# A gMLP/Hyena encoder block on one core: skip taps in fp32r, adaLN work of the filter stage on GpSimd and ScalarE, low halves on VectorE, and two output groups evicted tile by tile

## The chip, the cores and the metric

The kernel runs on 1 core of one Trainium2 chip. The metric is device time in microseconds (us) of one execution. Engine names are those of the profile: PE is TensorE's matmul (PEld its weight load), DVE is VectorE, ACT is ScalarE, POOL is GpSimd, SP is SyncE, which only issues DMAs here. A few DMAs are issued from ACT's queue.

## The reference

One layer on x of 512 x 2048, float32:

```
mod = SiLU(c) @ W_ada + b_ada -> sh1, sc1, g1, sh2, sc2, g2      (adaLN)
h   = x * (1 + sc1) + sh1
z   = h @ W_in + b_in      -> gMLP u, v | Hyena v, x1, x2 | gates a, b
A   = gMLP spatial gating of (u, v);  B = Hyena: y = x2 * (h2 * (x1 * (h1 * v)))
mix = (sigmoid(g_a) * (A @ W_a) + sigmoid(g_b) * (B @ W_b)) @ W_o + b_o
x   = LN(alpha * x + g1 * mix)
x   = LN(alpha * x + g2 * MLP_relu2(x * (1 + sc2) + sh2))
```

The Hyena's long filters h1, h2 (two directions each) come from a small network: two layers with Sin on 33 features, a third layer w3, a decay window. They are applied as convolutions by Fourier transforms; each filter has a `skip` term that is added to its first tap.

## The kernel before, in words

**Precision by pairs.** A large product is made of three fp32r matmuls: every operand is split into a high part (rounded to fp32r by a copy on ACT) and a low part (the difference, a subtraction on DVE): hi x hi, hi x lo, lo x hi. `split` (L74) does both halves. Weights come in blocks of 128x1024 (`wraw`), go through a ring of three buffers, and are split by `Weights.cast` (L164, ACT) and `Weights.finish` (L169, DVE). A dense group is eight blocks of 24 matmuls; before each block it takes a split pair of the ring, after each block it runs the functions listed for that block in `stages`.

**The order of work** is written out by hand: every engine runs its instructions in the order of the program, and waits where an operand is missing. An instruction that waits holds up all that is queued behind it on its engine.

**The opening (0 to about 190 us)** holds three threads, interwoven.

1. *adaLN vectors.* `Modulation` streams W_ada in 192 raw blocks of 128x1024. `step` (L289) is one DVE instruction per block: multiply by SiLU(c) (`cond`) and sum into `dots`. Four blocks give the shift and scale of one 128-row slice of the input; `load` asks for a further block with each step. The first 64 blocks are needed in the opening.
2. *The input.* After every fourth step `first_input` (L471) adds up `mod` (two tiny sums, L295 and L296, on POOL), makes the high part and the full value of h for this slice on ACT (L476, L477), and the low part on POOL (L478). Sixteen slices make h.
3. *The filters.* After the two Sin layers (`Sine`, `ready`) a loop of eight parts runs `taps(n+1)` (12 fp32r matmuls, L435, and in every second part one fp32 matmul with one row, `first_tap` x `skip`, L437), `transform(n)` (six fp32 matmul products, L338), two adaLN steps, `windowed(n+1)` (four DVE products that read PSUM, L445), the splitting of the next w3 half (`parts`), and the transform's `sums` (six DVE operations). `busy` puts dummy transposes on PE: 10, then 14 and 14 in the opening.

Then the first two dense groups of W_in (Hyena's v) run interleaved in 16 rounds: adaLN steps (44 in 13 rounds), `weights.finish` for the block of the next round, 24 matmuls, `weights.cast`.

**The output projection (from 1128 us).** Groups 0 and 1 of w_o (512 columns each) run on all four tiles of 128 tokens, groups 2 and 3 first on the two early tiles, then on the two late ones. `token_dense` returns four (or two) PSUM banks of eight; `gated_1` (L957) evicts each tile with three DVE operations (L960 times the gate row, L961 into the residual, L962 statistics) after the group's last matmul.

Of the kernel before, what the change touches and what calls it, by code (L numbers as in the profile page):

```python
# [18 lines left out]
P = 128  # L19
# [21 lines left out]
def block_kernel(ctx: ExitStack, tc: tile.TileContext, t):  # L41
# [25 lines left out]
    def f32(ap):  # L67
        return ap.bitcast(F32)
# [184 lines left out]
    nc.gpsimd.memset(sign[HID:], -1.0)  # L253
    first_tap = const.tile([1, P], F32, name="first_tap")
    nc.gpsimd.memset(first_tap, 0.0)
    nc.gpsimd.memset(first_tap[:, 0:1], 1.0)
    ident = const.tile([P, P], F32, name="ident")
# [12 lines left out]
    class Modulation:  # L270
        def __init__(self, order, room=lambda: 0):

            self.order, self.raw, self.room = [(m, kc, h) for m, kc in order for h in range(2)], [], room

        def load(self):
            early = sum(r[0] for r in self.raw)
            more = early < min(self.room(), 8)
            if self.order and (more or len(self.raw) - early < 3):
                m, kc, h = self.order.pop(0)
                if more:  # L280
                    raw = actp.tile([P, 1024], F32, name="araw", tag="act")
                else:
                    raw = wts.tile([P, 1024], F32, name="araw", tag="araw")
                load(raw, t["ada"][m, kc, h])
                self.raw.append((more, raw, m, kc, h))

        def step(self):
# [3 lines left out]
            if len(self.raw) < 11:  # L291
                self.load()

    def mod_sum(m, kc, eng=nc.vector):
# [91 lines left out]
    class Filters:  # L386
# [6 lines left out]
        def middle(self):  # L393
            x = self.one.reduce()
            nc.scalar.activation(x, x, AF.Sin)
            self.two = Sine(hw2, x, 1, P)

        def ready(self):

            x = self.two.reduce()  # L400
            nc.scalar.activation(x, x, AF.Sin)
            even, odd = slot_pair("a2e"), slot_pair("a2o")
            split(x, *even)
            for a, b in zip(even, odd):
                nc.scalar.activation(b, f32(a), AF.Identity, scale=sign)
            self.a2 = [[a.rearrange("h (p k) -> h k p", k=4) for a in pair] for pair in (even, odd)]

        def fetch(self, n):

            o, hf, cs = PARTS[n]  # L410
            if cs == 0:
                w = load(slot("w3"), t["w3"][o, hf].rearrange("d h c -> (d h) c"))
                skip = load(slot("skip")[:1], t["skip"][o, hf:hf + 1])
                self.raw.append((w, skip))
            if n in (0, 2):
# [3 lines left out]
        def parts(self, n):  # L419
            if PARTS[n][2] == 0:  # L420
                w, skip = self.raw.pop(0)
                both = slot_pair("w3")
                split(w, *both)
                self.w.append((*both, skip))

        def taps(self, n):

            cs = PARTS[n][2]
            wh, wl, skip = self.w[0] if cs == 0 else self.w.pop(0)
            ah, al = self.a2[cs]  # L430
            for cl in range(4):
# [4 lines left out]
                if extra:  # L436
                    nc.tensor.matmul(ps, first_tap, skip, start=False, stop=True)  # L437
                self.ps.append(ps)
# [31 lines left out]

    def first_input(kc, xt):  # L471

        mod_sum(slice(0, 2), kc, nc.gpsimd)
        hi, lo = act_pair(kc)
        sc, sh = mod[:, 1, kc:kc + 1], mod[:, 0, kc:kc + 1]
        nc.scalar.activation(hi, xt, AF.Identity, bias=sh, scale=sc)  # L476
        nc.scalar.activation(xt, xt, AF.Identity, bias=sh, scale=sc)  # L477
        nc.gpsimd.tensor_tensor(lo, xt, f32(hi), op=OP.subtract)  # L478
        h1.append((hi, lo))
# [22 lines left out]
    flt = Filters()  # L502
    flt.fetch(0)
    silu = [slot("silu") for _ in range(4)]
    quarters = [cond[:, 512 * h:512 * (h + 1)] for h in range(4)]
# [14 lines left out]

    def ada_steps(n):

        for _ in range(n):
            ada.step()
            done.append(None)
            if len(done) % 4 == 0:
                first_input(len(h1), xt[len(h1)])
                x_load()

    x_load()  # L530
# [4 lines left out]
    busy(14)  # L535
    ada_steps(2)
    flt.parts(0)
    flt.ready()
    busy(14)
    x_load()  # L540
    for _ in range(5):
        ada.load()
    flt.taps(0)
    ada_steps(2)
    flt.windowed(0)
    weights.later, weights.queue = [], nc.scalar
    for n in range(8):
        if n < 6 and n % 2 == 0:
            flt.fetch(n + 2)
        if n < 7:  # L550
            flt.taps(n + 1)
        sums = flt.transform(n)
        ada_steps(2)
        if n < 7:
            flt.windowed(n + 1)
        flt.store()
        if n < 6:
# [471 lines left out]
    def norm_stages(tiles, first):  # L1029

        out = {first: [lambda: mom[tiles].append(moments(st1, tiles)), do(normal_1, mom[tiles], tiles, 0)]}
        for k in range(1, 4):
# [3 lines left out]
    residual_load(0)  # L1036
    gated_1(token_dense(w_o, 0, 8, mp, stages={1: [gate_rows], 3: [gate_loads], 4: [do(residual_load, 1)],
                                               5: [do(residual, 0)]}), 0)
    gated_1(token_dense(w_o, 1, 8, mp, stages={0: [do(residual, 1), do(residual_load, 2)], 3: [do(residual, 2)],
                                               4: [do(residual_load, 3)], 6: [do(residual, 3)]}), 1)  # L1040
    for tiles in (early, late):
        for c in (2, 3):
# [5 lines left out]
            elif tiles is late:  # L1048
                stages = {1 + n: [do(second_input, early, 2 * n, held)] for n in range(7)}
            gated_1(token_dense(w_o, c, 8, mp, tiles, stages), c, tiles)  # L1050

# [187 lines left out]
```

## Time and profile before

| | |
|---|---|
| median of 3 runs | 2732.48 us (2732.22 to 2733.73) |
| profiled execution: time, span | 2733.2 us, 2731.4 us |
| mean granted TensorE clock | 0.996 |
| PE busy | 2688.6 us (98%) |
| DVE busy | 1539.5 us (56%) |
| ACT busy | 777.8 us (28%) |
| POOL busy | 118.8 us (4%) |
| DMA | 400.49 MB, mean 147 GB/s |

A line of the profile names the start, the length, the engine, the line of the kernel (L435), the operation, and what is written from what, with shapes. A bracket at the end gives the idle time of the engine before it and what ended it. Busy times of PE include time in which a matmul waits in its pipeline, so PE's start times, one after another, tell more than its share. The chain of waits follows the work that ended last back to the start.

### The profile page before, as it was taken

The numbers are of one execution on the slowest core, as the hardware profiler recorded it, in microseconds if no ns is written. First come the engines' busy times: TensorE is split into PE (matmuls) and PEld (weight loads), VectorE is DVE, ScalarE is ACT, GpSimd is POOL, SyncE is SP. The second block draws the span as 40 slices with busy tenths as digits, with TensorE's granted clock in tenths as the row PEclk, the third lists the DMA queues.
The fourth block names the chain that finished last, engine by engine and source line by source line (L and its number), as shares of the span: only waits on it lengthen the run. The fifth ranks groups of instructions, "written<-read, shape, count | busy, mean of one in ns | idle before, by whom it ended". The sixth has DMA issues, their size and how long they took to land.

```text
span 2731.4 us, 30019 instructions
## 1 busy us (share of the span) xinstructions
PE 2688.6 (98%) x12019; PEld 2210.1 (81%) x12019; DVE 1539.5 (56%) x2052; ACT 777.8 (28%) x949; POOL 118.8 (4%) x102
## 2 busy tenths in 40 slices
PE   8999999999999999999999999999999999999996
PEld 5678778888888888878988888888888888888885
DVE  8987989544575566456774343443433434334348
ACT  2343332222232222324621222312223222131232
POOL 0330000000000000140010000000000000000001
PEclk9999999999999999999999999999999999999998
DMA  9762333555665567445543222322223222223342
GB/s 346 300 242 84 118 113 135 196 190 196 200 209 186 198 220 258 156 152 177 183 134 100 94 100 93 101 93 100 94 99 97 96 100 93 101 92 101 95 140 82
DMA packets 120189, 400.49 MB, mean 147 GB/s; under 512 B 14187, under 2 KB 14283, under 8 KB 119920
## 3 DMA queue, kind: packets, MB, share of 16 engines
q1 hardware_dynamic: 116656, 387.26, 41.9%
q10 hardware_dynamic: 3392, 11.31, 1.1%
q8 instruction: 94, 1.54, 0.2%
q14 instruction: 47, 0.39, 0.0%
HBM read 388.01 MB, written 10.50 MB: 146 GB/s over the span
## 4 chain that ended last, share of the span: by engine, by line
PE 91%; DVE 5%; DMA 3%; issue 1%; ACT 1%; SPq 0%; DVEq 0%; ACTq 0%
PE d L207 57%; PE t L952 29%; DMA araw<-in_ada 2%; PE flt L435 1%; PE f_o L338 1%; DVE wlo L169 1%; DMA spec<-spec 1%; PE inv L703 1%; PE inv L690 1%; DMA wraw<-in_w_m 0%; PE f L342 0%; DVE araw L289 0%; DVE r L1104 0%; DVE r L968 0%; PE tr L609 0%
## 5 line engine op out<-in xcount | busy, mean ns | idle before, releaser
L207 PE MATMUL d<-act,whi 128*128 128x512 f32 (+1 forms) x4224 | 1273.1, 384 | 0.0
L169 DVE TENSOR_TENSOR wlo<-wraw,whi 128x1024 fp32r<-128x1024 f32 x480 | 589.0, 1229 | 993.2 <-ACT whi L164 989.9
L164 ACT CAST whi<-wraw 128x1024 fp32r<-128x1024 f32 x480 | 504.9, 1053 | 1488.2 <-PE d L207 873.2
L207 PEld LDWEIGHTS d<-act,whi 128*128 128x128 f32 x4224 | 783.1, 188 | 155.6 <-issue 2.4
L207 PE MATMUL d<-act,wlo 128*128 128x512 f32 (+1 forms) x2112 | 810.2, 384 | 10.2 <-DVE wlo L169 10.2
L207 PEld LDWEIGHTS d<-act,wlo 128*128 128x128 f32 x2112 | 396.7, 188 | 93.3 <-DVE wlo L169 15.9
L952 PE MATMUL t<-whi,fh 128*128 128x512 f32 x960 | 373.5, 389 | 0.0
L952 PE MATMUL t<-wlo,fh 128*128 128x512 f32 x960 | 373.5, 389 | 0.0
L952 PE MATMUL t<-whi,fl 128*128 128x512 f32 x960 | 373.5, 389 | 0.0
L289 DVE SCALAR_TENSOR_TENSOR araw<-araw,cond 128x1024 f32<-128x1024 f32 x192 | 238.6, 1259 | 7.8 <-DMA araw<-in_ada 7.6
L952 PEld LDWEIGHTS t<-whi,fl 128*128 128x128 f32 x960 | 180.2, 188 | 37.4
L952 PEld LDWEIGHTS t<-whi,fh 128*128 128x128 f32 x960 | 180.2, 188 | 37.4
L952 PEld LDWEIGHTS t<-wlo,fh 128*128 128x128 f32 x960 | 180.2, 188 | 37.4
L952 PE MATMUL t<-whi,act 128*128 128x512 f32 x512 | 159.7, 391 | 0.0
L952 PEld LDWEIGHTS t<-whi,act 128*128 128x128 f32 x512 | 96.1, 188 | 19.9
L967 DVE TENSOR_TENSOR gated<-t,cond 128x512 f32<-128x512 f32 x126 | 86.2, 684 | 31.6 <-PE t L952 31.6
L952 PE MATMUL t<-wlo,act 128*128 128x512 f32 x256 | 99.8, 390 | 2.1 <-DVE wlo L169 2.1
L968 DVE TENSOR_TENSOR r<-r,gated 128x512 f32<-128x512 f32 x126 | 87.2, 692 | 4.3
L207 PE MATMUL d<-whi,act 128*128 128x512 f32 x256 | 79.0, 389 | 0.0
L1062 DVE TENSOR_TENSOR relu<-relu 128x512 f32<-128x512 f32 (+1 forms) x68 | 45.6, 671 | 38.2 <-ACT fh L1061 38.2
L1106 POOL TENSOR_TENSOR r<-r,ln2b 128x512 f32<-128x512 f32 x6 | 10.0, 1665 | 1305.1 <-DVE r L1104 1303.8
L952 PEld LDWEIGHTS t<-wlo,act 128*128 128x128 f32 x256 | 48.1, 188 | 12.3 <-DVE wlo L169 2.5
(253 smaller groups left out, 1966.9 us busy)
## 6 DMA issues: line engine op xcount, KB each, us to landing
wraw<-in_w_m SPq DMA_DIRECT2D x264, 512.0 KB, 3.5
araw<-in_ada SPq DMA_DIRECT2D x192, 512.0 KB, 5.7
wraw<-in_w_in SPq DMA_DIRECT2D x123, 512.0 KB, 3.6
wraw<-in_w_o SPq DMA_DIRECT2D x48, 512.0 KB, 3.4
spec<-spec SPq DMA_DIRECT2D x48, 256.0 KB, 4.0
wraw<-in_w_in ACTq DMA_DIRECT2D x21, 512.0 KB, 6.7
wraw<-in_w_b SPq DMA_DIRECT2D x16, 512.0 KB, 3.6
wraw<-in_w_a SPq DMA_DIRECT2D x16, 512.0 KB, 3.4
```

The lines of the kernel that those rows point to most:

```text
L164: nc.scalar.copy(hi, raw)
L169: nc.vector.tensor_tensor(lo, raw, f32(hi), op=OP.subtract)
L207: nc.tensor.matmul(out[i], a, b, start=first and m == 0, stop=last and m == 2)
L289: nc.vector.scalar_tensor_tensor(raw, raw, 1.0, cond[:, 1024 * h:1024 * (h + 1)], op0=OP.mult, op1=OP.mult, accum_out=dots[:, m, kc, h:h + 1])
L338: nc.tensor.matmul(ps, fc(k), x, start=first, stop=last)
L435: nc.tensor.matmul(ps, a[:, cl, :], w, start=m == 0, stop=m == 2 and not extra)
L690: nc.tensor.matmul(ps, ic(4 * cs + COLUMN[cl]), y[cl][cs], start=(cs == 0), stop=(cs == 1))
L703: nc.tensor.matmul(ps[:, cl * P:(cl + 1) * P], conv.y[cl][cs][:, s], ic(4 * cs + COLUMN[cl]), start=(cs == 0), stop=(cs == 1))
L952: nc.tensor.matmul(out[i], a, b, start=kc == 0 and m == 0, stop=kc == 2 * pairs - 1 and m == 2)
L967: nc.vector.tensor_tensor(x, ps[i], g2_row[c], op=OP.mult)
L968: nc.vector.tensor_tensor(r[i][c], r[i][c], x, op=OP.add)
L1062: nc.vector.tensor_tensor(x, x, x, op=OP.mult)
```

## The change

In the opening:

- `first_tap` becomes a one-hot of 97 rows in fp32r; the four skip rows are loaded once, into rows 0, 32, 64 and 96 of one tile, split (`skips`), and each is added by two fp32r matmuls with one row instead of one fp32 matmul.
- `Modulation` gets a second way to handle a block: `products` multiplies on POOL, `add_up` sums on ACT. In the filter loop the two DVE steps of each part are gone; two or three blocks go the new way (19 in all). Before the loop four DVE steps and two products stand ahead of the first windows, where two steps stood. 25 of the 64 blocks are done when the loop ends (20 before), 39 are left for the 13 rounds.
- The low part of h moves from POOL to DVE, put off (`lows`, `low`) until after the next adaLN step, or in the loop until after the windows. In the loop the two tiny sums are made on DVE.
- The last Sin is computed twice on ACT (once rounded, once in full) instead of copied, its range reduction stands earlier, and the second and third `busy` are 14 and 36.

In the output projection the four tiles of group 0 are evicted as stages of group 1 (after blocks 0, 2, 4, 6), and those of group 1 as stages of group 2 of the early tiles.

```diff
@@ -251,9 +251,13 @@
     nc.gpsimd.memset(sign[HID:], -1.0)
-    first_tap = const.tile([1, P], F32, name="first_tap")
-    nc.gpsimd.memset(first_tap, 0.0)
-    nc.gpsimd.memset(first_tap[:, 0:1], 1.0)
+    first_tap = const.tile([97, P], F32R, name="first_tap")
+    one_hot = small.tile([97, P], F32, name="one_hot", tag="one_hot")
+    nc.gpsimd.memset(one_hot, 0.0)
+    nc.gpsimd.memset(one_hot[:, 0:1], 1.0)
+    nc.vector.tensor_copy(first_tap, one_hot)
+    skip_raw = slot("skip")[:97]
+    nc.gpsimd.memset(skip_raw, 0.0)
     ident = const.tile([P, P], F32, name="ident")
@@ -270,12 +274,12 @@
-            self.order, self.raw, self.room = [(m, kc, h) for m, kc in order for h in range(2)], [], room
+            self.order, self.raw, self.half, self.room = [(m, kc, h) for m, kc in order for h in range(2)], [], [], room
         def load(self):
-            early = sum(r[0] for r in self.raw)
+            early = sum(r[0] for r in self.raw + self.half)
             more = early < min(self.room(), 8)
-            if self.order and (more or len(self.raw) - early < 3):
+            if self.order and (more or len(self.raw + self.half) - early < 3):
                 m, kc, h = self.order.pop(0)
@@ -290,6 +294,22 @@
                 self.load()
+
+        def products(self, n):
+
+            for _ in range(n):
+                _, raw, m, kc, h = item = self.raw.pop(0)
+                nc.gpsimd.tensor_tensor(raw, raw, cond[:, 1024 * h:1024 * (h + 1)], op=OP.mult)
+                self.half.append(item)
+
+        def add_up(self):
+            n = len(self.half)
+            while self.half:
+                _, raw, m, kc, h = self.half.pop(0)
+                nc.scalar.activation(raw, raw, AF.Copy, accum_out=dots[:, m, kc, h:h + 1])
+                if len(self.raw) < 11:
+                    self.load()
+            return n
@@ -395,12 +415,15 @@
+        def reduced(self):
+            self.x = self.two.reduce()
+
         def ready(self):
-            x = self.two.reduce()
+            x, even, odd = self.x, slot_pair("a2e"), slot_pair("a2o")
+            nc.scalar.activation(even[0], x, AF.Sin)
             nc.scalar.activation(x, x, AF.Sin)
-            even, odd = slot_pair("a2e"), slot_pair("a2o")
-            split(x, *even)
+            nc.vector.tensor_tensor(even[1], x, f32(even[0]), op=OP.subtract)
             for a, b in zip(even, odd):
@@ -409,24 +432,26 @@
             if cs == 0:
-                w = load(slot("w3"), t["w3"][o, hf].rearrange("d h c -> (d h) c"))
-                skip = load(slot("skip")[:1], t["skip"][o, hf:hf + 1])
-                self.raw.append((w, skip))
+                self.raw.append(load(slot("w3"), t["w3"][o, hf].rearrange("d h c -> (d h) c")))
             if n in (0, 2):
...
             if PARTS[n][2] == 0:
-                w, skip = self.raw.pop(0)
                 both = slot_pair("w3")
-                split(w, *both)
-                self.w.append((*both, skip))
+                split(self.raw.pop(0), *both)
+                self.w.append(both)
+
+        def skips(self):
+            self.skip = [x[:97] for x in slot_pair("skip")]
+            split(skip_raw, *self.skip)
...
-            cs = PARTS[n][2]
-            wh, wl, skip = self.w[0] if cs == 0 else self.w.pop(0)
+            o, hf, cs = PARTS[n]
+            wh, wl = self.w[0] if cs == 0 else self.w.pop(0)
+            row = 32 * (2 * o + hf)
             ah, al = self.a2[cs]
@@ -434,7 +459,8 @@
                 if extra:
-                    nc.tensor.matmul(ps, first_tap, skip, start=False, stop=True)
+                    for m, x in enumerate(self.skip):
+                        nc.tensor.matmul(ps, first_tap[row:row + 1], x[row:row + 1], start=False, stop=m == 1)
                 self.ps.append(ps)
@@ -468,14 +494,20 @@
-    def first_input(kc, xt):
-
-        mod_sum(slice(0, 2), kc, nc.gpsimd)
+    lows = []
+
+    def low():
+        while lows:
+            lows.pop(0)()
+
+    def first_input(kc, xt, eng):
+
+        mod_sum(slice(0, 2), kc, eng)
         hi, lo = act_pair(kc)
...
         nc.scalar.activation(xt, xt, AF.Identity, bias=sh, scale=sc)
-        nc.gpsimd.tensor_tensor(lo, xt, f32(hi), op=OP.subtract)
+        lows.append(lambda: nc.vector.tensor_tensor(lo, xt, f32(hi), op=OP.subtract))
         h1.append((hi, lo))
@@ -501,6 +533,8 @@
     flt.fetch(0)
+    for k in range(4):
+        load(skip_raw[32 * k:32 * k + 1], t["skip"][k // 2, k % 2:k % 2 + 1])
     silu = [slot("silu") for _ in range(4)]
@@ -518,14 +552,21 @@
+    def counted(n, eng):
+
+        for _ in range(n):
+            done.append(None)
+            if len(done) % 4 == 0:
+                first_input(len(h1), xt[len(h1)], eng)
+                x_load()
+
     def ada_steps(n):
-
+        if not n:
+            low()
         for _ in range(n):
             ada.step()
-            done.append(None)
-            if len(done) % 4 == 0:
-                first_input(len(h1), xt[len(h1)])
-                x_load()
+            low()
+            counted(1, nc.gpsimd)
@@ -533,26 +574,34 @@
     busy(14)
-    ada_steps(2)
+    ada_steps(1)
+    flt.reduced()
     flt.parts(0)
+    ada_steps(1)
     flt.ready()
-    busy(14)
+    flt.skips()
+    busy(36)
     x_load()
...
     ada_steps(2)
+    ada.products(2)
+    ada_steps(2)
+    low()
     flt.windowed(0)
...
             flt.fetch(n + 2)
+        counted(ada.add_up(), nc.vector)
         if n < 7:
...
         sums = flt.transform(n)
-        ada_steps(2)
         if n < 7:
+            ada.products(2 + n % 2)
             flt.windowed(n + 1)
+        low()
         flt.store()
@@ -1034,10 +1083,11 @@
     residual_load(0)
-    gated_1(token_dense(w_o, 0, 8, mp, stages={1: [gate_rows], 3: [gate_loads], 4: [do(residual_load, 1)],
-                                               5: [do(residual, 0)]}), 0)
-    gated_1(token_dense(w_o, 1, 8, mp, stages={0: [do(residual, 1), do(residual_load, 2)], 3: [do(residual, 2)],
-                                               4: [do(residual_load, 3)], 6: [do(residual, 3)]}), 1)
+    ps_0 = token_dense(w_o, 0, 8, mp, stages={1: [gate_rows], 3: [gate_loads], 4: [do(residual_load, 1)],
+                                              5: [do(residual, 0)]})
+    ps_1 = token_dense(w_o, 1, 8, mp, stages=merged(
+        {0: [do(residual, 1), do(residual_load, 2)], 3: [do(residual, 2)], 4: [do(residual_load, 3)], 6: [do(residual, 3)]},
+        {2 * i: [do(gated_1, ps_0, 0, (i,))] for i in TILES}))
     for tiles in (early, late):
@@ -1047,6 +1097,8 @@
                 stages = {1 + n: [do(second_input, early, 2 * n, held)] for n in range(7)}
+            elif c == 2:
+                stages = {2 * i: [do(gated_1, ps_1, 1, (i,))] for i in TILES}
             gated_1(token_dense(w_o, c, 8, mp, tiles, stages), c, tiles)
```

## The prediction

> **What bounds the kernel now.** I read the page first, for the span and the chain of waits; then the busy time by stretch of the opening, where the chain leaves the matmuls; then the order of time of each engine there.
>
> ```profile
> span 2731.4 us, 30019 instructions
> ...
> PE 91%; DVE 5%; DMA 3%; issue 1%; ACT 1%; SPq 0%; DVEq 0%; ACTq 0%
> ```
>
> The profiled execution took 2733.2 us, 1.8 more than its span and 0.7 more than the median of the runs, 2732.48; sums are made against 2733.2 and 0.7 is taken off at the end. PE holds 91% of the chain. An edit can pay only where PE stands still, and the diff touches two such places: the first 190 us and the passage from the second to the third group of w_o. A measurement of this kernel can tell about 0.2%, 5.5 us, from no change.
>
> ```profile
> 20.00:40.00 20.00, 20.00 (x54) 12.97 (x54) 17.08 (x29) 3.86 (x6) 1.94 (x5) 0.83 1.03 404
> 40.00:60.00 20.00, 20.00 (x58) 11.90 (x57) 19.63 (x34) 5.32 (x8) 1.79 (x4) 1.00 0.92 333
> 80.00:100.00 20.00, 18.41 (x60) 11.22 (x58) 19.93 (x34) 4.69 (x6) 1.70 (x3) 1.00 0.31 101
> 100.00:120.00 20.00, 18.74 (x80) 14.93 (x81) 20.00 (x27) 6.97 (x9) 9.86 (x9) 1.00 1.03 410
> ```
>
> The columns that matter are PE, DVE, then the granted clock, the DMA share and GB/s. In the filter stage (20 to 92 us) PE is full and DVE nearly so; in the stage of the first two dense groups (from 92 us) DVE is full at 20.00 and PE loses 1.26 us in 20. The clock is low once, 0.83 in the first stretch.
>
> ```profile
> 12.31 4.27 PE L264 MATMUL busy<-ident 128*128 128x128 f32 x28
> 19.60 0.62 PE L435 MATMUL flt<-w3h,a2eh 128*128 128x512 f32 x1 [3.03 <-ACT a2eh L76]
> ...
> 25.33 0.63 PE L435 MATMUL flt<-w3h,a2eh 128*128 128x512 f32 x1
> 25.76 0.63 PE L435 MATMUL flt<-w3l,a2eh 128*128 128x512 f32 x1
> ...
> 28.43 0.40 PE L435 MATMUL flt<-w3h,a2ol 128*128 128x512 f32 x1
> 28.67 0.40 PE L435 MATMUL flt<-w3h,a2oh 128*128 128x512 f32 x1
> ...
> 30.08 1.02 PE L338 MATMUL f_ee<-flt,fwd 128*128 128x512 f32 x2
> ...
> 36.02 1.12 PE L437 MATMUL flt<-skip,first_tap 1*128 1x512 f32 x2
> 37.08 0.62 PE L435 MATMUL flt<-w3h,a2eh 128*128 128x512 f32 x1
> ...
> 39.43 1.02 PE L338 MATMUL f_ee<-flt,fwd 128*128 128x512 f32 x2
> ...
> 47.40 1.02 PE L338 MATMUL f_ee<-flt,fwd 128*128 128x512 f32 x2
> ...
> 88.88 3.60 PE L338 MATMUL f_o<-flt,fwd 128*128 128x512 f32 x8
> ```
>
> First transform at 30.08, last one ended at 92.5, and PE was never free between: the filter stage is bound by PE. Two iterations take 17.3 us (30.08 to 47.40), of which the skip term with its fp32 matmuls at K=1 costs 1.4 (9.35 against 7.97 us). After 3.03 us idle PE ran matmuls 0.43 us apart instead of 0.24; a clock of 0.83 over 20 us is 6.8 us at half rate, and the spacing is whole again by 28.4, so it began about a microsecond after the work did.
>
> **Step 1, up to the first transform.**
>
> ```profile
> 12.42 0.78 ACT L312 ACTIVATE sine<-flt,hfb,c_hcol 128x512 f32<-128x512 f32 x1 [2.16 <-PE flt L311]
> ...
> 18.93 0.62 ACT L76 CAST a2eh<-sine 128x512 fp32r<-128x512 f32 x1
> 19.64 0.73 ACT L405 ACTIVATE a2oh<-a2eh,sign 128x512 fp32r<-128x512 f32 x1
> ```
>
> ```profile
> 14.13 0.68 DVE L77 TENSOR_TENSOR w3l<-w,w3h 128x512 fp32r<-128x512 f32 x1
> 14.73 0.41 DVE L316 TENSOR_SCALAR sine_k<-sine 128x512 f32<-128x512 f32 x1
> ...
> 17.81 0.43 DVE L320 TENSOR_SCALAR sine<-sine 128x512 f32<-128x512 f32 x1
> ...
> 20.19 1.22 DVE L289 SCALAR_TENSOR_TENSOR araw<-araw,cond 128x1024 f32<-128x1024 f32 x1
> ...
> 21.33 1.22 DVE L289 SCALAR_TENSOR_TENSOR araw<-araw,cond 128x1024 f32<-128x1024 f32 x1
> ```
>
> ```profile
> 6.25 0.29 SPq L71 DMA_DIRECT2D skip<-in_skip  x1
> ```
>
> The sine's argument is there at 13.2 (12.42+0.78), where the new order starts the reduction (3.5 us, 14.73 to 18.24): 16.7. Then on DVE the filter weights' low half, 0.6: 17.3; one adaLN step, 1.15 (20.19 to 21.33): 18.5; the low half of the sine, 0.6: 19.1. The second Sin on ACT replaces a copy and hides here. On SP three more rows of skip (0.29 each) go ahead of the first loads of x and adaLN weights, 0.9 us; what they push back is first used after 20 us, so nothing (end: 0.9). The skip rows' split is new: on ACT behind two operations of 0.73 it ends at 20.5, on DVE at 21.1. PE is filled by 14+36 dummy transposes at 0.1525 us (4.27/28) from 12.31 to 19.9, so the first 24 tap matmuls run at 0.24 us and end at about 26.3, not 30.08. That gain is lost again, since the transform needs the windowed taps, and on DVE these now stand behind four adaLN steps and the low half of the first input, where two steps stood.
>
> ```profile
> 102.22 1.11 POOL L295 TENSOR_TENSOR mod<-dots 128x2 f32<-128x2 f32 x1 [5.87 <-DVE araw L289]
> ...
> 106.26 1.60 POOL L478 TENSOR_TENSOR act<-xT,act 128x512 fp32r<-128x512 f32 x1 [1.78 <-ACT xT L477]
> ...
> 173.25 1.11 POOL L295 TENSOR_TENSOR mod<-dots 128x2 f32<-128x2 f32 x1 [1.32 <-DVE araw L289]
> 174.44 0.20 POOL L296 TENSOR_TENSOR mod<-mod,c_bada 128x2 f32<-128x2 f32 x1
> 176.41 1.29 POOL L478 TENSOR_TENSOR act<-xT,act 128x512 fp32r<-128x512 f32 x1 [1.78 <-ACT xT L477]
> ```
>
> ```profile
> 96.35 1.22 DVE L289 SCALAR_TENSOR_TENSOR araw<-araw,cond 128x1024 f32<-128x1024 f32 x1
> ...
> 106.64 2.31 DVE L289 SCALAR_TENSOR_TENSOR araw<-araw,cond 128x1024 f32<-128x1024 f32 x1
> ```
>
> Three DVE steps end at 24.5. The low half then waits for POOL's sums and two ACT passes: POOL's second sum runs about 24.8 to 25.0, and from there the row 174.44 to 176.41 gives 1.77 us: 26.7. POOL meanwhile multiplies: a 128x512 product is 1.29, so 2.6 for 1024 columns, 25.0 to 27.6. The DVE step at 106.64 lasted 2.31 us instead of 1.22 because POOL held 106.26 to 107.86; both read two operands from SBUF. So I let the low half end at 28.2, the second product at 30.8, the fourth step at 31.95, the first window at 32.55. First transform at 32.6 against 30.08: +2.5; its second product needs the third window, +0.35. If nothing contended, the window would end at 29.1, a gain of 1.0; these are the ends.
>
> PE then idles from 26.3 to 32.6. Before, a shorter idle brought 6.8 us of half clock, starting some 1.3 us after work resumed, 4.3 us after the idle began. From 26.3 that is 30.6 to 37.4, of which 4.8 us have work, so 2.4 us are lost; ends 0 and 3.4. The Trainium skill, "TensorE: Matmul & The Clock Gate", Part 1, What's actually happening, gives one busy window of about 3.4 us until the clock returns; by it the loss would be 1.7 us, an estimate. The row of before shows a longer stretch, and the sum goes by the row.
>
> **Step 2, the filter loop.** Three skip terms remain in it. Two fp32r matmuls at 0.24 should cost about 0.5 where 1.4 stood: 3 x 0.9, a gain of 2.7 (ends 0, if the K=1 rows bring the gap with them, and 2.8). The adaLN work that leaves DVE was beside a full PE and pays nothing by itself: DVE loses four steps per pair, 4.6 of 17.0 us (19.63 of 20 over 17.3), and gets sums and a low half, some 1.3: 13.7 against 16.4 of PE. POOL's 19 products (49 us) and ACT's 19 accumulations (an ACT pass of 512 columns is 0.62, so 1.25 each, 24 us) fit in 62 us and run an iteration ahead. On DVE the mod sums wait for these accumulations; windows, splits and sums are queued behind them and PE behind those, but they are early. Where DVE's splits with two SBUF operands meet POOL's products they wait up to 2.6 each; 2.7 per pair is free. I add 0.5 (ends 0 and 3.6). The loop therefore ends at +2.5+0.35+2.4-2.7+0.5, about 3.0 us later.
>
> **Step 3, the first two dense groups.**
>
> ```profile
> 173.16 1.15 DVE wlo L169
> ...
> 219.35 5.44 PE d L207 x24
> ```
>
> A PE block of 24 matmuls is 5.45 us; DVE sets the pace. Before, DVE went from 96.35 (first step after the last sums) to 173.16 (the weight split for block 13), 76.8 us, with 44 adaLN steps and 11 collisions like that at 106.64. Now 39 steps are left, as 25 are done in the loop, not 20: 39 x 1.15 = 44.7; twelve weight splits, 13.7. POOL's low half goes to DVE, 0.6, nine times. It is queued behind only one further step, and all weight splits behind it: the row pair 173.25 and 176.41 puts the operand 3.3 us after the fourth step (which ended just before 173.1), 1.15 of which are covered, so DVE stands 2.1 us; where a weight split lies between, POOL's second sum collides too (102.22 to 106.26, 4.2 us with 2.3 covered): 1.9. Nine times 2.65: 23.9. Together 82.3, +5.5. Against this, the last two steps of the loop no longer stand ahead of its last sums: these end 1.3 us after PE's last transform instead of 3.9 (92.5 and 96.35): -2.6 to -2.7. Net +2.8. The low end: if the wait were hidden, 64 us of DVE work would be left, PE's 13 blocks (70.9) would bound, and the step would give -8.6. DMA carries five loads fewer in this stage, and 4.4 transfers per block in 6.4 us, under the 410 GB/s it has shown; its 31% in 80 to 100 stays, since the loads hang on the same consumed buffers.
>
> **Step 4, the evictions of w_o.**
>
> ```profile
> 1213.68 0.69 DVE L960 TENSOR_TENSOR gated<-t,g1row 128x512 f32<-128x512 f32 x1 [1.09 <-PE t L952]
> ...
> 1222.16 3.48 DVE L169 TENSOR_TENSOR wlo<-wraw,whi 128x1024 fp32r<-128x1024 f32 x3
> ```
>
> ```profile
> 1139.48 74.18 PE t L952 x327
> ```
>
> ```profile
> 1223.42 0.50 PE L952 MATMUL t<-wlo,act 128*128 128x512 f32 x1 [2.07 <-DVE wlo L169]
> ```
>
> Twelve DVE operations stood between 1213.7 and 1222.2, 8.5 us, ahead of the weight splits; blocks of the early half take 2.7 us (half of 5.45), two are ready, and PE stood 2.07 us plus some 0.2 to refill. Spread at every second block, DVE has 2.1 of eviction and two splits of 1.15 in 5.4 us: the stall goes, and nothing is late next, as the free time is 1 us per pair. Group 0's eviction lies within 74.18 us of the chain that are PE alone, so nothing is to be had there. All eight banks are in use in the second group, but the first are released before the third asks. Step: -2.3 (ends 0 and -2.5).
>
> **Sum.** 3.0 + 2.8 - 2.3 = +3.5: 2736.7 beside 2733.2, so 2736.0 as a median.
>
> **Rival 1, the relief of DVE counts (faster).** The waits for POOL and ACT are shorter than I read them, the low half finds its operand, and windows are not held: step 1 gives -1.0, step 2 -2.7, step 3 goes to PE's bound, -8.6, step 4 -2.3: 14.6 less, 2718; with half of step 3's wait left, about 2724. For it: DVE is full in the dense stage and PE waits on its splits. Against it: the chain from sum to operand is in every row of POOL. It needs both the gap of 2.1 us and the collisions to shrink. 0.2.
>
> **Rival 2, POOL's port becomes the bound of the filter loop (slower).** A low half and a weight split on DVE come back to back, and between them POOL's next product takes its turn: 1.3 and 2.6 us per pair on average. It decides from 2.7 us per pair, the free time above. Price: 1.2 to 2 us per pair, three pairs, and the second weight split, needed by the taps behind the first transform, late by some 3 us: 6.6 to 9 over the forecast, about 2743.5. For it: the row at 106.64, and products that fill four fifths of the loop. Against: operations with a PSUM operand are not held, and they are most of DVE's work here. 0.27.
>
> **Rival 3, the evictions only move.** If the stages delay the splits as much as the block did, step 4 is 0: 2738.3. The 1 us spare speaks against it. 0.08.
>
> **How the numbers follow.** The forecast has 0.45. Same means 2727.0 to 2738.0. The forecast lies in it save for its upper end (0.40 same, 0.03 slower, 0.02 faster), rival 3 halves, rival 2 is slower all but 0.02, rival 1 is faster all but 0.03: faster 0.19, same 0.49, slower 0.32. The range 2722 to 2746 takes in the bounds of the clock and the collisions, rival 2 and the nearer half of rival 1.
>
> **What would show it.** Right: a PE gap of about 6 us before the first transform and a granted clock below 1 there; the last transform ending at about 95; DVE idle some 2 us before each low half after it; block 13's split at about 180; no stall near 1220. Wrong: DVE without those gaps, taps held by the weight split, or fp32r skip terms that cost over 1 us.

## The result, and the profile after

The changed kernel took 2758.99 us (median of four runs, 2757.93 to 2759.51), the kernel before 2733.11 beside it: ratio 1.0092, 95% interval 1.0074 to 1.0109, so slower by 0.9%. The profiled execution took 2759.51 us, its span 2757.7 (2731.4 before): 26.3 us to be found. First the page: its span, and the chain of waits by engine.

```profile
span 2757.7 us, 30062 instructions
...
PE 88%; DVE 6%; DMA 3%; issue 1%; ACT 1%; POOL 0%; SPq 0%; DVEq 0%; ACTq 0%; POOLq 0%
```

PE's share of the chain fell from 91% to 88% and DVE's rose from 5% to 6%. Busy time by stretch of the changed kernel (PE, PE's weight loads, DVE, ACT, POOL, then granted clock, DMA share, GB/s) shows where:

```profile
20.00:40.00 20.00, 12.38 (x33) 8.02 (x33) 18.30 (x16) 4.75 (x8) 16.00 (x8) 0.83 1.03 406
40.00:60.00 20.00, 14.35 (x30) 7.49 (x29) 16.83 (x20) 7.87 (x14) 19.86 (x9) 0.74 0.55 204
60.00:80.00 20.00, 16.36 (x43) 10.47 (x42) 18.66 (x22) 5.26 (x10) 10.13 (x5) 0.84 0.58 206
80.00:100.00 20.00, 20.00 (x57) 11.96 (x57) 16.47 (x29) 12.51 (x20) 2.37 (x1) 0.99 0.83 291
```

Where PE was full before, it now loses 17 of 60 us, at a granted clock of 0.74 to 0.84, for as long as POOL is busy. From 80 us on, with POOL nearly done, PE is full. PE in order of time in the changed kernel:

```profile
34.52 2.07 PE L358 MATMUL f_ee<-flt,fwd 128*128 128x512 f32 x2 [7.15 <-DVE flt L471]
...
48.66 0.82 PE L460 MATMUL flt<-w3l,a2eh 128*128 128x512 f32 x1 [4.56 <-DVE w3l L77]
...
55.01 1.79 PE L358 MATMUL f_ee<-flt,fwd 128*128 128x512 f32 x2
...
63.74 1.02 PE L358 MATMUL f_ee<-flt,fwd 128*128 128x512 f32 x2
...
72.93 0.63 PE L460 MATMUL flt<-w3l,a2eh 128*128 128x512 f32 x1 [3.64 <-DVE w3l L77]
...
78.92 1.79 PE L358 MATMUL f_ee<-flt,fwd 128*128 128x512 f32 x2
...
87.65 1.02 PE L358 MATMUL f_ee<-flt,fwd 128*128 128x512 f32 x2
...
93.03 0.40 PE L460 MATMUL flt<-w3l,a2eh 128*128 128x512 f32 x1
...
96.60 1.02 PE L358 MATMUL f_ee<-flt,fwd 128*128 128x512 f32 x2
...
111.42 3.60 PE L358 MATMUL f_o<-flt,fwd 128*128 128x512 f32 x8
```

The first transform begins at 34.52 (30.08 before, +4.4). The next follows after 20.5 us where 9.35 stood (+11.1), the fourth after 15.2 (+5.8); both times the taps wait for the low half of the filter weights, and run 0.43 us apart behind the wait, where 0.24 is usual. Once POOL is done, a part with a skip term takes 8.95 us (87.65 to 96.60), 0.4 less than before. The last transform ends at 115.0 (111.42 + 3.60), 92.5 before: **22.5 of the 26.3 us are lost in the filter stage.** What held the low half, on DVE and on POOL of the changed kernel:

```profile
24.65 3.17 DVE L293 SCALAR_TENSOR_TENSOR araw<-araw,cond 128x1024 f32<-128x1024 f32 x1 [0.81 <-DMA araw<-in_ada]
...
33.78 2.47 DVE L471 TENSOR_TENSOR flt<-flt,win 128x512 f32<-128x512 f32 x4
36.18 2.21 DVE L315 TENSOR_TENSOR mod<-dots 128x2 f32<-128x2 f32 x1
38.42 2.27 DVE L316 TENSOR_TENSOR mod<-mod,c_bada 128x2 f32<-128x2 f32 x1
40.61 2.47 DVE L471 TENSOR_TENSOR flt<-flt,win 128x512 f32<-128x512 f32 x4
43.01 2.85 DVE L510 TENSOR_TENSOR act<-xT,act 128x512 fp32r<-128x512 f32 x1
45.78 2.82 DVE L77 TENSOR_TENSOR w3l<-w,w3h 128x512 fp32r<-128x512 f32 x1
```

```profile
24.35 40.67 POOL L302 TENSOR_TENSOR araw<-araw,cond 128x1024 f32<-128x1024 f32 x16
```

Sixteen products follow each other almost without a gap, 2.54 us each on average. Every DVE instruction in that time whose two operands both lie in SBUF ends about its own running time after the end of a product: the step takes 3.17 instead of 1.22, the low halves 2.8 instead of 0.7, and the two additions of 256 numbers over 2.2 each (0.16 when POOL is idle). The wait goes both ways. Eleven of the sixteen products took 2.35 to 2.40 us; the other five, each the next in turn behind a stretched step or low half, took 2.78 to 3.33. The windows, with one operand in PSUM, are not stretched (0.6 each).

In the dense stage of the changed kernel DVE shows the forecast wait, and block 13's split:

```profile
134.73 0.69 DVE L510 TENSOR_TENSOR act<-xT,act 128x512 fp32r<-128x512 f32 x1 [2.06 <-ACT xT L509]
...
200.12 1.22 DVE L169 TENSOR_TENSOR wlo<-wraw,whi 128x1024 fp32r<-128x1024 f32 x1
```

Its first step is at 118.70, so 81.4 us to block 13's split (76.8 before); the split is 27.0 later than before, 4.4 more than the loop's 22.5. In the output projection, the chain of the changed kernel is PE without a break past the second group:

```profile
1156.46 10.88 PE t L1001 x48
...
1167.45 92.75 PE t L1001 x409
```

The same place in the kernel before:

```profile
1128.49 10.88 PE t L952 x48
```

Group 0 begins at 1156.46 (1128.49 before) and the span ends 1601.2 us later, not 1602.9: the evictions give 1.7 back. With 1.0 us between block 13 and group 0 that I did not follow, 22.5 + 4.4 + 1.0 - 1.7 is the 26.3.

### The profile page after: what moved, and what is told of

The parts are those of the page before. It is cut to its first block, busy times and chain, and to the rows that moved or that the text cites. A ratio compares the mean times of both kernels' runs of the same rounds, so it can differ in the third digit from the quotient of the medians.

```text
span 2757.7 us, 30062 instructions
## 1 busy us (share of the span) xinstructions
PE 2698.0 (98%) x12041; PEld 2216.5 (80%) x12041; DVE 1544.8 (56%) x2042; ACT 798.4 (29%) x988; POOL 133.2 (5%) x96
## 4 chain that ended last, share of the span: by engine, by line
PE 88%; DVE 6%; DMA 3%; issue 1%; ACT 1%; POOL 0%; SPq 0%; DVEq 0%; ACTq 0%; POOLq 0%
PE d L207 55%; PE t L1001 28%; DVE wlo L169 1%; DVE araw L293 1%; PE flt L460 1%; DMA araw<-in_ada 1%; PE f_o L358 1%; PE inv L752 1%; PE inv L739 0%; DMA xT<-in_xT 0%; DMA wraw<-in_w_in 0%; DMA wraw<-in_w_m 0%; PE f L362 0%; DVE act L510 0%; DVE r L1156 0%
## 5 line engine op out<-in xcount | busy, mean ns | idle before, releaser
L207 PEld LDWEIGHTS d<-act,wlo 128*128 128x128 f32 x2112 | 397.1, 188 | 96.9 <-DVE wlo L169 19.1
L293 DVE SCALAR_TENSOR_TENSOR araw<-araw,cond 128x1024 f32<-128x1024 f32 x173 | 212.9, 1243 | 6.1 <-DMA araw<-in_ada 5.9
```

The costliest lines, as they stand in the source:

```text
L207: nc.tensor.matmul(out[i], a, b, start=first and m == 0, stop=last and m == 2)
L293: nc.vector.scalar_tensor_tensor(raw, raw, 1.0, cond[:, 1024 * h:1024 * (h + 1)], op0=OP.mult, op1=OP.mult, accum_out=dots[:, m, kc, h:h + 1])
```

## The experiments

The theory: POOL's reads hold the port that DVE's second SBUF operand needs, and a few DVE instructions on the way to the filter weights' low half are made to wait one product each. The rivals: the products are simply too much work in the wrong place; the late first transform and the clock are carried along; the transfers.

**The evictions alone** (the kernel before with only the last hunk of the diff).

> The kernel before with the evictions of groups 0 and 1 as stages and nothing else of the change. Theory (the evictions help, the opening costs all): 1.7 to 2.1 us less than before, about 2731, and no wait of TensorE for a weight split in the third group. Rival (the evictions only move the delay): no change, and the wait of 2.07 us is found at another block.

2731.78 us against 2734.54, ratio 0.9989 (0.9979 to 0.9998); span 2728.8, 2.6 less than before. From the second to the third group the chain of this kernel has no DVE in it, where 8.5 us stood:

```profile
1127.62 10.88 PE t L952 x48
...
1138.61 117.21 PE t L952 x516
```

From group 0 to the end it takes 1601.2 us, 1.7 less, as in the changed kernel. This part of the change holds. The other 0.9 of the 2.6 lies ahead of group 0, where the code is that of the kernel before: the first transform began at 28.65, not 30.08. So one execution can differ from another by more than a microsecond in the opening.

**The products on DVE**, in the same places.

```diff
-                nc.gpsimd.tensor_tensor(raw, raw, cond[:, 1024 * h:1024 * (h + 1)], op=OP.mult)
+                nc.vector.scalar_tensor_tensor(raw, raw, 1.0, cond[:, 1024 * h:1024 * (h + 1)], op0=OP.mult,
+                                               op1=OP.mult, accum_out=dots[:, m, kc, h:h + 1])
...
-                nc.scalar.activation(raw, raw, AF.Copy, accum_out=dots[:, m, kc, h:h + 1])
```

> The changed kernel, but the 19 blocks that GpSimd multiplies and ScalarE adds up are done by VectorE's one instruction, at the same places. Theory (GpSimd's products hold the port that VectorE's two-operand instructions need): VectorE gets 22 us more work and the loop still ends 11 to 14 us earlier, at 101 to 104 instead of 114.9; 2745 to 2748 in all; no VectorE instruction of the loop is stretched. Rival (the order of the work and the chain over ScalarE cost the time, not the port): with more work on VectorE the loop ends no earlier, 2759 or more.

2747.51 us, ratio 1.0045 (1.0028 to 1.0062), 11.5 less than the changed kernel although DVE has more to do; the loop ends at 99.8, 15.2 earlier. On DVE of this kernel:

```profile
31.93 0.15 DVE L315 TENSOR_TENSOR mod<-dots 128x2 f32<-128x2 f32 x1
...
37.48 0.68 DVE L77 TENSOR_TENSOR w3l<-w,w3h 128x512 fp32r<-128x512 f32 x1
```

So these instructions are not stretched, and most of the loss goes with the engine. The loop still ends 7.3 us later than before the change; DVE's larger load and the place of the work may share that, which no run here separates. This kernel also does without ACT's passes over the 19 blocks; the next one keeps them.

**POOL only writes.**

```diff
-                nc.gpsimd.tensor_tensor(raw, raw, cond[:, 1024 * h:1024 * (h + 1)], op=OP.mult)
+                for _ in range(3):
+                    nc.gpsimd.memset(raw, 0.0)
```

> The changed kernel, with each product on GpSimd replaced by three memsets of the same tile, some 2.7 us that only write (the adaLN sums of these blocks are left out, so its output is not the reference's). Theory (the port, held while GpSimd reads): no VectorE instruction of the loop is stretched, the loop ends near 90, 2734 in all. Rival (GpSimd's time itself, by way of ScalarE's sums): unchanged, 2759 and a loop that ends near 115.

2742.5 us (one execution), span 2740.4, loop end 96.9; it leaves out the products. POOL, DVE and ACT of this kernel:

```profile
24.02 32.13 POOL L303 MEMSET araw<- 128x1024 f32 x33
```

```profile
25.82 0.69 DVE L511 TENSOR_TENSOR act<-xT,act 128x512 fp32r<-128x512 f32 x1
...
31.14 0.16 DVE L316 TENSOR_TENSOR mod<-dots 128x2 f32<-128x2 f32 x1 [1.09 <-ACT araw L310]
```

```profile
37.08 0.62 ACT L76 CAST w3h<-w 128x512 fp32r<-128x512 f32 x1 [3.36 <-DMA w<-in_w]
```

POOL is as busy as ever (2.9 us a block), yet DVE runs at full speed beside it, and 18 of the 22.5 us are gone: most of the cost is POOL's reads, not its time. The Trainium skill, "SBUF — State Buffer", Who interferes with whom, says just this: a DVE instruction with two SBUF inputs contends with a GpSimd instruction that reads SBUF, not with one that only writes it. But I had expected the loop to end near 90. What is left lies between the first two transforms (16.4 us instead of 9.35), and the row on ACT names a transfer: the next filter weights.

**That load earlier**, in the kernel whose POOL only writes.

```diff
...
+    flt.fetch_w(2)
     for _ in range(5):
         ada.load()
```

> The kernel whose POOL only writes, with the load of the second filter weights put ahead of the five adaLN loads before the loop (leaves out the adaLN products of 19 blocks, as that kernel does). If its remaining 16.4 us between the first two transforms come from this load, which stands behind two more adaLN blocks in the queue and lands at about 36.9: the cast of the weights no longer waits, the interval falls to about 9, the half clock behind it goes too, last transform near 89, span near 2733.5 (2740.4 with the late load). Rival: ACT's sums hold ACT or DVE there whatever the load does; span within 1.5 of 2740.4.

Span 2734.1 (one execution), loop end 91.7. The cast waits no more, and the interval is 9.5 us. PE of this kernel:

```profile
29.98 1.12 PE L359 MATMUL f_ee<-flt,fwd 128*128 128x512 f32 x2 [1.99 <-DVE flt L477]
...
39.47 1.02 PE L359 MATMUL f_ee<-flt,fwd 128*128 128x512 f32 x2
```

So the change had a second cost, 5 us of loop: these weights are asked for at 27.04 in the kernel whose POOL only writes, and at 23.20 before the change. Two more adaLN blocks go into a full queue (406 GB/s) ahead of them, some 2.5 us; most of the rest stands already in the load of x ahead of those blocks (22.99, 21.91 before). In the changed kernel the cast does not wait for them: it stands on ACT behind two passes that wait for DVE's sums, and begins at 42.81.

**Products in halves** (`quarters` are the four 512-column parts of `cond`).

```diff
-                nc.gpsimd.tensor_tensor(raw, raw, cond[:, 1024 * h:1024 * (h + 1)], op=OP.mult)
+                for q in range(2):
+                    s = slice(512 * q, 512 * (q + 1))
+                    nc.gpsimd.tensor_tensor(raw[:, s], raw[:, s], quarters[2 * h + q], op=OP.mult)
```

> The changed kernel, with each product on GpSimd made in two halves of 512 columns. Theory (the port is held for a whole instruction): what the ten stretched VectorE instructions wait, about 2 us each, is halved; the loop ends 8 to 10 us earlier, 2749 to 2751. Rival (the port is shared by the bytes moved, or GpSimd's total time counts): unchanged, 2759.

2761.92 us, ratio 1.0099 (1.0084 to 1.0114): no gain, against the theory as I had it. The first waits did shrink (the sums took 1.2 to 1.3 us instead of 2.2 to 2.3), and the third transform began 12 us earlier than in the changed kernel. Then, on DVE, POOL and in the busy time of this kernel:

```profile
50.31 21.48 DVE L317 TENSOR_TENSOR mod<-dots 128x2 f32<-128x2 f32 x1
```

```profile
24.14 47.63 POOL L304 TENSOR_TENSOR araw<-araw,cond 128x512 f32<-128x512 f32 x36
```

```profile
60.00:80.00 20.00, 5.18 (x10) 3.04 (x11) 19.93 (x16) 4.71 (x8) 11.78 (x10) 0.52 0.15 48
```

One addition of 256 numbers is down as running for 21.48 us, until POOL's run of 36 halves was over (24.14 + 47.63 = 71.77); 17 halves began in that time. So DVE does not always get its turn after one POOL instruction. Why it missed it here and got it in the other cases, no run here shows.

**The sums back on POOL.**

```diff
-        counted(ada.add_up(), nc.vector)
+        counted(ada.add_up(), nc.gpsimd)
```

> The changed kernel, with the two mod sums of 128x2 in the filter loop back on POOL, behind its products. If DVE's loss is one turn of about 2.2 us at the port for every DVE instruction with two SBUF operands, whatever its size, then two turns go from each of two iterations (0.16 us lasted 2.2 to 2.3 us at 36.18, 38.42 and 62.74 us): the filter weights' low half ends 4 us earlier in both, the loop ends 6 to 9 us earlier, near 107, time 2750 to 2754. Rival: the loss is set by POOL's 19 products as a whole, or the sums on POOL come so late that the low half stalls DVE: no gain, 2757 or more.

2742.9 us (one execution), loop end 99.4: twice the gain expected, 15.6 us in the loop. On POOL of this kernel:

```profile
32.30 12.62 POOL L302 TENSOR_TENSOR araw<-araw,cond 128x1024 f32<-128x1024 f32 x5
47.97 0.20 POOL L315 TENSOR_TENSOR mod<-dots 128x2 f32<-128x2 f32 x1 [3.05 <-ACT araw L309]
```

The sums wait for ACT, and the products behind them too, so POOL's run breaks into groups of two and five, with 3 to 6 us of idle time ahead of the later ones. Two causes, then; the next kernel tells them apart.

**POOL waits, the sums stay on DVE**: one more addition on POOL in the same place.

```diff
...
         counted(ada.add_up(), nc.vector)
+        if len(h1) > seen:
+            seen, idle = len(h1), small.tile([P, 2], F32, name="idle", tag="idle")
+            nc.gpsimd.tensor_tensor(idle, dots[:, 0:2, seen - 1, 0], dots[:, 0:2, seen - 1, 1], op=OP.add)
```

> The changed kernel with its two sums still on DVE, and beside them one more 128x2 addition of the same numbers on POOL into a scratch tile, at the place where the kernel with the sums on POOL has them. So POOL must wait for ACT's accumulations before it goes on with its products, and its run of 16 in a row breaks into groups, while DVE's sums stay exposed. If that run is what held DVE (an instruction of DVE waits for as long as products follow each other), most of the 16 us that the sums on POOL brought come back: loop end near 100 to 104, span 2741 to 2746. Rival: the moved sums themselves were the gain (three turns of 2.2 us and the half clock behind them): loop end 110 or later, span 2752 to 2758.

Span 2754.9 (one execution), loop end 110.3: 4.7 us of the 15.6. POOL's run breaks into the same groups, with up to 11 us of idle time between. The sums are still held, and the low half behind them. DVE of this kernel:

```profile
57.83 2.17 DVE L315 TENSOR_TENSOR mod<-dots 128x2 f32<-128x2 f32 x1
60.04 2.27 DVE L316 TENSOR_TENSOR mod<-mod,c_bada 128x2 f32<-128x2 f32 x1
```

So the breaks in POOL's run are the smaller part; the other 10.9 us came with moving two sums per slice, 0.3 us of work, off DVE.

**The first windows earlier**, ahead of products, steps and low half.

```diff
     ada_steps(2)
+    flt.windowed(0)
     ada.products(2)
     ada_steps(2)
     low()
-    flt.windowed(0)
```

> The changed kernel with the first windows moved ahead of the two POOL products, two adaLN steps and the low half that stand before them. If the loop is paced by DVE's chain at the port (stretched steps, low half, sums, windows of part 1, low half of the filter weights at 45.8 to 48.5), the first transform comes 6 to 8 us earlier (34.5 in the changed kernel) and that is all: the second one stays near 55, the loop end near 115, time 2756 to 2760. Rival: the late first transform and the half clock behind it are carried through the loop: the second transform 5 to 8 us earlier, time 2751 to 2754.

2754.1 us (one execution), loop end 109.0. PE of this kernel:

```profile
27.09 1.02 PE L358 MATMUL f_ee<-flt,fwd 128*128 128x512 f32 x2
...
41.09 0.82 PE L460 MATMUL flt<-w3h,a2eh 128*128 128x512 f32 x1 [8.69 <-ACT w3h L76]
...
52.62 1.47 PE L358 MATMUL f_ee<-flt,fwd 128*128 128x512 f32 x2
```

The first transform comes 7.4 us earlier, of which 2.4 are left at the second: DVE's chain sets that one (the weights' low half begins at 43.40, 2.4 earlier). That the time still falls by 5 us is the rival's number; 2.9 of it come later, where DVE met the products at other moments (61.04 to 73.31, 12.3 us, where the changed kernel has 15.2). The run settles the first interval, not the whole.

**The low half three steps late** in the dense stage.

```diff
             ada.step()
-            low()
+            if len(done) % 4 == 3:
+                low()
             counted(1, nc.gpsimd)
```

> The changed kernel, but outside the filter loop the low half on DVE is emitted three adaLN steps after its operand was asked for, not one step. If step 3 was right (DVE stands about 2 us before each of nine or ten low halves in the dense stage, and that stage is paced by DVE), the gaps of 1.8 to 2.1 us ahead of the low half are gone there, the split for block 13 comes 7 to 11 us earlier (200.1 in the changed kernel, less 18 us of waits, but not under PE's 13 x 5.45 us), and the time is 2749 to 2752. Rival: the stage is paced by the transfers (their share is 0.88 to 0.93 there), and the time moves by less than 3 us. The filter loop should be as in the changed kernel, its last transform ending near 115.

2745.58 us, ratio 1.0037 (1.0023 to 1.0051): 13.4 less than the changed kernel, more than expected. Busy time of this kernel, in the stage where the changed one has PE at 17 to 18 of 20:

```profile
140.00:160.00 20.00, 20.00 (x90) 16.57 (x89) 20.00 (x32) 8.68 (x10) 4.92 (x6) 1.00 1.00 388
```

PE is full, block 13's split is at 185.0 (15.1 earlier), and DVE's gaps ahead of the low halves are gone: step 3's mechanism. The loop's last transform ends at 114.1, so 70.9 us lie between it and the split (80.7 before), the 70.9 that the low end of step 3 gave to PE's 13 blocks.

**No products at all**: DVE steps as before the change, the low half late, the rest of the change kept.

```diff
...
         sums = flt.transform(n)
+        ada_steps(2)
         if n < 7:
-            ada.products(2 + n % 2)
             flt.windowed(n + 1)
-        low()
...
```

> The changed kernel without POOL products and ACT sums: two adaLN steps on DVE in each part of the loop, at the place where the kernel before had them, and two steps ahead of the first windows; the low half on DVE, three steps late; evictions, skip rows in fp32r, dummy work and the double Sin as in the changed kernel. If the port was the loss and the rest of the change is worth what its steps say: first transform near 27.5 (30.08 in the kernel before), loop end near 90, no stretched DVE instruction in the loop, the low half no longer stretching an adaLN step by 1.09 us in the dense stage (some 5 us), evictions 2.7: 2720 to 2726, under both kernels. Rival: the dense stage of the kernel before is paced by its transfers (410 GB/s) and the loop by DVE with the low halves added: then only the evictions and part of the opening stay, 2729 to 2732.

2738.95 us, ratio 1.0015 (1.0006 to 1.0024): not faster than before, outside both expectations. The first transform came early, as expected; the rest in PE and busy time of this kernel:

```profile
26.91 1.02 PE L358 MATMUL f_ee<-flt,fwd 128*128 128x512 f32 x2
...
104.99 0.79 PE L207 MATMUL d<-act,wlo 128*128 128x512 f32 x1 [5.29 <-DVE wlo L169]
```

```profile
80.00:100.00 20.00, 19.70 (x64) 12.33 (x62) 19.90 (x33) 5.79 (x8) 0.78 (x2) 1.00 0.12 34
100.00:120.00 20.00, 15.01 (x59) 12.24 (x59) 20.00 (x32) 5.14 (x6) 4.40 (x6) 0.83 1.03 408
```

With the low halves added, DVE is full at the end of the loop and starts the dense stage late: its first step there is 6.5 us behind the last transform (3.9 before). Loads that hang on its steps leave the queue nearly idle (34 GB/s) and then crowd it (408), and DVE waits 6.2 us for adaLN blocks in that stage (2.4 before). How the loss is shared between the two is not shown. So the relief of DVE by POOL seems to be worth something after all.

**Two repairs**: the change, with the sums on POOL and the low half late.

> The changed kernel with the mod sums of the loop on POOL and the low half of the dense stage three steps late, so the two edits that each took 13 to 16 us off alone (2742.9 and 2745.6 against 2759). If they mend different stages, the sum holds: loop end near 99, dense stage paced by PE's 5.2 to 5.7 us a block, 2728 to 2731, under the kernel before. Rival: what one mends lets the transfers become the bound of the dense stage, as in the kernel with all blocks on DVE (2739.0): 2734 to 2740.

2727.72 us, ratio 0.9974 (0.9964 to 0.9984): faster than the kernel before by 7 us. The two gains add up (16.1 and 13.4 alone, 31.3 together). Busy time of this kernel:

```profile
100.00:120.00 20.00, 19.67 (x87) 15.97 (x86) 19.57 (x31) 7.94 (x10) 5.39 (x6) 1.00 1.02 382
120.00:140.00 20.00, 20.00 (x90) 16.56 (x89) 20.00 (x32) 8.76 (x11) 4.92 (x6) 1.00 1.01 378
```

The loop ends at 97.5, 5 us later than before the change, but the dense stage is now bound by PE.

**Four repairs**: besides, the first windows and the filter weights' load earlier.

> As the kernel with two repairs, and besides the first windows ahead of the products and the second filter weights' load ahead of five adaLN loads. First transform near 27.5 (32.4 with the sums on POOL), no half clock behind it, second transform near 38 to 40 (44.2), loop end near 93 to 95: 2721 to 2726. Rival: DVE's chain of stretched instructions, not the start, sets the second transform: within 2 us of the kernel with two repairs.

2727.87 us, ratio 0.9977 (0.9968 to 0.9986): the rival's number. The first transform is at 27.24, the second at 44.10 (43.77 with two repairs). Its taps still wait for DVE, as these rows of PE show, the first of this kernel, the second of the one with two repairs:

```profile
37.75 0.82 PE L465 MATMUL flt<-w3l,a2eh 128*128 128x512 f32 x1 [2.32 <-DVE w3l L77]
```

```profile
39.98 0.63 PE L460 MATMUL flt<-w3l,a2eh 128*128 128x512 f32 x1 [0.58 <-DVE w3l L77]
```

DVE's chain alone does not set the second transform, though. The low half is there 2.2 us earlier, but behind the wait the taps are 0.43 us apart and take 6.35 us to the transform, where they took 3.79 with two repairs: the low clock behind PE's idle time uses the gain up.

## Why the prediction was wrong

**Step 1 held in kind.** The gap ahead of the first transform was there (7.15 us; forecast 6.3), the transform 4.4 later (forecast 2.5), as three stretched DVE instructions, not two, stood ahead of the windows. The third is the step at 24.65: it waited 0.81 us for its adaLN block, and so came behind the first product (24.35) instead of ahead of it. The forecast held that the skip rows' loads push back nothing that matters. SP of the changed kernel:

```profile
7.87 3.81 SPq L71 DMA_DIRECT2D skip<-in_skip  x4
```

Four rows took SP 3.81 us, not 0.29 each, and the first load of x came 3.0 us later than before (11.73 against 8.73). That this made the step wait is likely, but no run has the rows loaded another way. The clock fell as forecast: the granted clock was 0.50 from about 32.7 to 39.5 us, 6.8 us as before the change, and some 2.5 us were lost from 34.52 on (an estimate; forecast 2.4). That loss was hidden: the second transform waited for DVE anyway.

**Step 2 failed**, at the sentence "I add 0.5 (ends 0 and 3.6)". From the first transform to the end of the last the forecast had 0.55 us more than before (0.35 + 2.4 - 2.7 + 0.5); it took 18.1 more. Three things were missing. The list of DVE instructions that meet the products held the splits but not the two small sums, which I took as part of "sums and a low half, some 1.3" us; yet an addition of 256 numbers waited 2.1 us, as long as a step of 128x1024 did (1.95 and 2.14 us beyond its 1.22). The waits were set against the mean free time of a pair, 2.7 us, while they fall in a row ahead of one consumer: sums, low half and weights' low half are late by 4.1, 2.1 and 2.1 us in a single iteration. And both PE gaps in the loop brought half clock behind them: from 48.66 to 55.01 the taps took 6.35 us, where the same ones took 3.57 later (93.03 to 96.60). The skip terms gave 0.4 each, not 0.9.

**Rival 2 was what happened**, but its price of 6.6 to 9 us over the forecast is less than half of the 19.5 by which the loop ended later than forecast (115.0 against 95.5); it too left out the sums and the clock.

**Step 3 held on DVE**: waits of 1.8 to 2.1 us ahead of eight of the nine low halves (0.65 at the other), 81.4 us against 82.3 forecast. The 2.6 us expected from the earlier start did not come: the loop's last sums stand behind a low half that waits 1.78 us itself, and DVE's first step is 3.7 us behind the last transform (3.9 before). Net +4.4, forecast +2.8. That stage's low end, which the forecast had only as part of rival 1 (0.2), was one edit away, as the kernel with the low half three steps late shows.

**Step 4 held**: -1.7 against -2.3, shown by the kernel with the evictions alone.

## What to carry to other kernels

Before work goes to POOL, list every DVE instruction with two SBUF operands that will run beside it, the tiny ones too, and charge each with a whole POOL instruction (once here it was the rest of POOL's run); then see which of them stand one behind the other ahead of a single consumer. An operand that another engine finishes late should be consumed as many instructions later as its chain is long: here three steps later was worth 13 us. And look at parts one by one: this change was 26 us slower as a whole and 7 faster with two of its lines altered.

## What the runs showed of the hardware

- Additions of 128x2 on DVE took 0.16 us beside an idle or only writing POOL, and up to 2.3 beside POOL products that took 2.35 to 2.40 us where nothing held them up.
- A POOL product behind a DVE step that had waited took 3.3 us, and behind a low half that had waited 2.8, instead of 2.4: each engine holds up the other.
- Beside POOL products of 128x512, 1.3 us each, one such addition took 21.48 us, to the end of POOL's run. The Trainium skill, "SBUF — State Buffer", Who interferes with whom, says that only the shared port pair causes contention and that it is an exclusive lock; that the loser can miss turn after turn, only this run shows.
- POOL's memsets of 128x1024 took 0.97 us each (three made up a block) and did not slow DVE's two-operand instructions.
- Two fp32r matmuls with one row stood 0.33 us apart from each other and their neighbours at full clock, 0.6 at half clock; a part with them took 0.4 us less than one with a single fp32 matmul in their place.
